# Three late quads instead of four, column ranges of 512, half-block tiles, and a scale moved to GpSimd

## The chip, the cores and the metric

The kernel runs on one core of a Trainium2 chip. The metric is the device time of one execution in microseconds. Each comparison is between medians of several runs; the profile is one further execution, taken by the hardware profiler, and its time is given beside its span.

## The reference

The layer takes 256 positions of width 2048 in float32. What matters here is its second half:

```
hn = rmsnorm(x)                                   # 256 x 2048
x += hier_moe(hn)                                 # 32 experts, each position uses 2 of one group of 8
     # expert e: (silu(xs @ Wg) * (xs @ Wu)) @ w_down[e], w_gate_up[e] 2048 x 1024, w_down[e] 512 x 2048
x += sigmoid(rmsnorm(x) @ w_ple_gate) * (p @ w_ple_proj)      # w_ple_gate 2048 x 2048
y  = rmsnorm(x) * g_final
```

The first half (input projection, attention, short convolution, two branches, output projection) is not touched. All 32 experts' weights are read from memory: 256 MiB of gate/up and 128 MiB of down weights.

## The kernel before, in words

The program is written in engine order by hand: each engine runs its instructions as the Python code issues them, and all weights are fetched by DMAs that SyncE (SP) issues in that order. A load waits on SP until the block of memory that it goes to has been read out by its last user, and every later load waits behind it.

Memory is a set of blocks of 1 MiB (8 KB on each of 128 partitions), named b0 to b25. A list `free` holds those that serve as a rotating ring for weight tiles; `rot_blk` takes the next one, `retire` takes blocks out of the ring for another use.

Experts are worked in quads of four, 32 slots each, so that one quad fills 128 rows (`experts`, line 893). For each expert the gate/up product (`gate_up`, L813) reads 8 tiles of 1 MiB, and `hidden` (L821 to L826) makes the hidden values. In an early quad, `down` (L834) at once reads the expert's four 1 MiB down tiles, and `combine` (L848, L849) places the quad's rows back on the positions and adds them to `x2`. In a late quad (`LATE`, quads 4 to 7) only the hidden values are kept (`tail["hs"]`), with the matrix that places them (`SwT`, in `tail["st"]`); the down products follow in `late_stage` (line 1001).

`late_stage` works by ranges of columns of `x2`, `CHUNKS`: 0 to 1023, 1024 to 1535, 1536 to 2047. For a range, `down_part` loads pieces of w_down for four experts (L1009) and multiplies (L1017), `place` adds the result to `x2` (L1035, L1036), and `prep` (L1050, L140 to L144) transposes the finished columns and splits them into a high and a low part. The range is then a slice of the contraction of `x2 @ w_ple_gate` (class `Gemm`, L262 to L264, three products for each of the two parts). The gate weights are loaded in tiles of four contraction blocks (L230), each split in two halves of two blocks (L140 on ScalarE, L141 on VectorE) into four blocks b14 to b17. `run(n)` issues n such halves, each with the splits for the half three places ahead; 12 matmuls make a half. While one range is multiplied, the down pieces of the next are brought in between the halves.

Quads 4 and 5 (`WIDE`) load pieces of two blocks by 1024 columns, quads 6 and 7 (`FINE`) the same up to column 1023 and pieces of four blocks by 512 columns from there on. All are 1 MiB, and so are most gate tiles.

In the last range the output of the product comes in five lots of columns (three of 512, two of 256). For each lot and both halves of the positions (`g_evac`, L976 to L987): add the sum of the earlier ranges, sigmoid on ScalarE, multiply by the projected embedding, add to `x2`, square on ScalarE for the last norm, and multiply by `g_final` (L987, on VectorE). `store` scales by the last norm's factor and writes out.

Of the kernel before, what the change touches and what calls it, by code (L numbers as in the profile page):

```python
# [37 lines left out]
def block_kernel(  # L38
# [163 lines left out]

    WIDE, FINE = (4, 5), (6, 7)
    LATE = WIDE + FINE
    ex1 = Experts(rot_blk, LATE)

    class Gemm:
        def __init__(self, spool, load):
            self.sp = spool
            self.load = load  # L210
            self.halves = []
            self.ns = 0
            self.nl = 0
            self.i = 0
            self.cur = {}
            self.look = LOOK
            self.feeds = False

        def add(self, src, col, n, ks, acts, evac, before=None):
# [4 lines left out]
        def load_to(self, j):  # L224
            while self.nl < min(j, len(self.halves)):
                src, col, n, ks, k, acts, evac, before, cell = self.halves[self.nl]
                kt = min(4 if n > 256 else 8, ks)
                if k % kt == 0:
                    w = self.load([P, kt, n])
                    SY.dma_start(out=w, in_=src[0, k * P:(k + kt) * P, col:col + n].rearrange(  # L230
                        "(k p) n -> p k n", p=P))
                    cell[k] = w
                self.nl += 1

        def split_to(self, j):
            self.load_to(j)
            while self.ns < min(j, len(self.halves)):
                src, col, n, ks, k, acts, evac, before, cell = self.halves[self.ns]
                kt = min(4 if n > 256 else 8, ks)
# [653 lines left out]
    def experts(ex, first):  # L893
        for q in range(8):
# [6 lines left out]
            for i in range(4):  # L901
# [3 lines left out]
                if first and e == 4 * LATE[0]:  # L905
                    retire(5, 7)
                    tail["hs"] = blk(5, [P, 4 * len(LATE), P])
                    tail["st"] = blk(7, [P, 2, 1024])
# [18 lines left out]
                if i == 0:  # L927
# [3 lines left out]
                    if late:  # L931
                        SwT = tail["st"][:, 0, (q - LATE[0]) * T:(q - LATE[0] + 1) * T]
                    else:
# [7 lines left out]

    CHUNKS = ((0, 1024), (1024, 512), (1536, 512))
    cx = {}

    def cact(c):
# [5 lines left out]
    def late_gate():  # L951
        gg = Gemm(sblk, rot_blk)
        z = []

        def g_evac(c, n, col, w):
            last = c == len(CHUNKS) - 1

            def f(ps):
# [41 lines left out]
    def late_stage(gg):  # L1000
        hs, st = tail["hs"], tail["st"]
        y4c = st[:, 1]
        py = {}

        def down_part(q, col, w, f0, nf):
            tiles = []
            for i in range(4):
                wt = rot_blk([P, nf, w])
                SY.dma_start(out=wt, in_=w_down[0, 4 * q + i, f0 * P:(f0 + nf) * P, col:col + w].rearrange(  # L1009
# [19 lines left out]
        def place(q, col, w):  # L1029
            SwT = st[:, 0, (q - LATE[0]) * T:(q - LATE[0] + 1) * T]  # L1030
            for b in range(w // 512):
# [6 lines left out]
        def prep(c):  # L1038
            o, w = CHUNKS[c]
            if c == 0:  # L1040
                cx[c] = (blk(4, [P, 8, T], FR), blk(Y4, [P, 8, T], FR))
            else:
                hl = blk((18, 4)[c - 1], [P, 2, 4, T], FR)
                cx[c] = (hl[:, 0], hl[:, 1])
            for k in range(0, w // P, 2):
# [22 lines left out]

        prev = None
        for q in LATE:  # L1070
            down_part(q, 0, 1024, 0, 2)
            if prev is not None:
                place(prev, 0, 1024)
            if q == LATE[-1]:
                gg.split_to(3)
            down_part(q, 0, 1024, 2, 2)
            prev = q
        place(prev, 0, 1024)
        prep(0)
        run(4)  # L1080
        for q in WIDE:
            down_part(q, 1024, 1024, 0, 2)
            run(2 if q == WIDE[0] else 1)
            down_part(q, 1024, 1024, 2, 2)
            run(1)
            place(q, 1024, 1024)
            run(1)
        for q in FINE:
            down_part(q, 1024, 512, 0, 4)
            run(1)  # L1090
            place(q, 1024, 512)
            run(1)
        run(15 - gg.i)
        prep(1)
        run(1)
        run(4)
        down_part(FINE[0], 1536, 512, 0, 4)
        run(1)
        place(FINE[0], 1536, 512)
        run(1)  # L1100
        down_part(FINE[1], 1536, 512, 0, 4)
        run(1)
        place(FINE[1], 1536, 512)
        run(1)
        prep(2)
        retire(6)
        gg.load_to(len(gg.halves))
# [127 lines left out]
```

## Time and profile before

| | |
|---|---|
| median of 3 runs | 1738.76 us (1735.45 to 1742.49) |
| profiled execution | 1737.67 us, span 1735.9 us |
| TensorE matmul busy | 1436.4 us, 83% of the span |
| VectorE, ScalarE busy | 594.9 us (34%), 419.9 us (24%) |
| GpSimd busy | 0.6 us |
| moved by DMA | 547.48 MB, mean 315 GB/s |
| chain that ended last | PE 48%, DMA 47% |

How to read it: the mean hides three stages. In the first 600 us TensorE is busy nearly throughout (591.72 of 600 us) and the DMAs move 202 GB/s; from there to the last gate/up product the DMAs are the busier ones; the late stage follows. Shares of a whole span say little about any of these. A matmul's busy time is modelled and pipelined, so the start times of successive rows tell more than the durations.

### The profile page before, as it was taken

What the parts mean: (1) busy time and instruction counts of PE and PEld (TensorE: products, weight loads), DVE (VectorE), ACT (ScalarE), POOL (GpSimd) and SP (SyncE); (2) the same over time, 40 slices, a digit from 0 to 9 for tenths busy, and PEclk for the clock granted to TensorE, in tenths of its full rate; (3) what the DMA queues carried; (4) which work ended last, traced back from release to release, by engine and by line L of the source; (5) the groups of instructions that cost most, each with busy time, mean ns of one, the idle gap of its engine ahead of it and who ended that gap; (6) DMA issues with size and microseconds to landing.
All of it is one profiled execution on the core that took longest, in us unless ns stands there. A gap on an engine that the chain in (4) does not pass through costs nothing.

```text
span 1735.9 us, 22289 instructions
## 1 busy us (share of the span) xinstructions
PE 1436.4 (83%) x9464; PEld 911.1 (52%) x9464; DVE 594.9 (34%) x940; ACT 419.9 (24%) x632; POOL 0.6 (0%) x6
## 2 busy tenths in 40 slices
PE   8999999999999997776676676777876766788993
PEld 6899888888888786332132141243443421134562
DVE  5545766554554544221021030110100100142456
ACT  6434444444444332100000000000100000031244
POOL 0000000000000000000000000000000000000000
PEclk9999999999999999998697797696888777989996
DMA  7656555555557768999999999999999999979961
GB/s 243 202 148 217 194 165 175 182 184 193 192 194 295 263 242 322 411 419 418 420 420 419 419 419 419 419 419 418 419 418 420 419 419 389 391 254 375 387 242 50
DMA packets 147838, 547.48 MB, mean 315 GB/s; under 512 B 13260, under 2 KB 24852, under 8 KB 106260
## 3 DMA queue, kind: packets, MB, share of 16 engines
q1 hardware_dynamic: 147344, 543.85, 81.6%
q10 hardware_dynamic: 388, 2.13, 0.3%
q8 instruction: 76, 1.25, 0.3%
q14 instruction: 30, 0.25, 0.0%
HBM read 543.84 MB, written 2.11 MB: 315 GB/s over the span
## 4 chain that ended last, share of the span: by engine, by line
PE 48%; DMA 47%; DVE 2%; ACT 1%; issue 1%; SPq 0%; ACTq 0%; DVEq 0%
DMA b<-in_w_gate_up_dram 30%; DMA b<-in_w_down_dram 16%; PE acc L262 13%; PE acc L264 13%; PE acc L263 13%; PE tmp L1017 3%; PE acc L813 2%; PE tmp L791 1%; DMA b<-in_w_ple_proj_dram 1%; PE tmp L1035 1%; DMA b<-in_x_dram 0%; PE tmp L655 0%; PE acc L834 0%; DVE b L793 0%; DVE b L984 0%
## 5 line engine op out<-in xcount | busy, mean ns | idle before, releaser
L813 PE MATMUL acc<-b,b 128*32 128x256 f32 x4096 | 325.4, 463 | 132.5 <-DMA b<-in_w_gate_up_dram 107.1
L262 PE MATMUL acc<-b,b 128*128 128x512 f32 (+2 forms) x1096 | 424.7, 388 | 4.7 <-ACT b L140 4.6
L263 PE MATMUL acc<-b,b 128*128 128x512 f32 (+2 forms) x1096 | 413.5, 377 | 1.6 <-DVE b L141 1.6
L264 PE MATMUL acc<-b,b 128*128 128x512 f32 (+2 forms) x1096 | 413.9, 378 | 0.0
L141 DVE TENSOR_TENSOR b<-b,b 128x1024 fp32r<-128x1024 f32 (+2 forms) x278 | 318.2, 1148 | 258.5 <-ACT b L140 257.8
L140 ACT ACTIVATE b<-b 128x1024 fp32r<-128x1024 f32 (+2 forms) x278 | 275.1, 995 | 294.6 <-PE acc L264 266.7
L813 PEld LDWEIGHTS acc<-b,b 128*32 128x32 f32 x4096 | 133.5, 127 | 310.5 <-DMA b<-in_w_gate_up_dram 187.3
L262 PEld LDWEIGHTS acc<-b,b 128*128 128x128 f32 x1096 | 207.3, 189 | 51.1 <-issue 8.7
L263 PEld LDWEIGHTS acc<-b,b 128*128 128x128 f32 x1096 | 207.4, 189 | 38.1 <-DVE b L141 2.3
L264 PEld LDWEIGHTS acc<-b,b 128*128 128x128 f32 x1096 | 207.0, 189 | 37.3 <-DVE b L144 0.2
L821 ACT ACTIVATE hh<-acc 128x128 f32<-128x128 f32 x32 | 8.9, 278 | 577.2 <-PE acc L813 340.6
L822 DVE TENSOR_TENSOR hh<-acc,hh 128x128 f32<-128x128 f32 x32 | 9.3, 291 | 395.6 <-ACT hh L821 395.6
L1017 PE MATMUL tmp<-b,b 128*32 128x512 f32 x512 | 99.7, 705 | 34.6 <-DMA b<-in_w_down_dram 34.6
L834 PE MATMUL acc<-b,hh 128*32 128x512 f32 x512 | 82.0, 757 | 25.8 <-DMA b<-in_w_down_dram 19.8
L791 PE MATMUL tmp<-SS,b 128*128 128x128 f32 x512 | 78.7, 310 | 10.4 <-DVE SS L782 10.4
L791 PEld LDWEIGHTS tmp<-SS,b 128*128 128x128 f32 x512 | 70.6, 215 | 27.4 <-DVE SS L782 12.8
L1017 PEld LDWEIGHTS tmp<-b,b 128*32 128x32 f32 x512 | 21.3, 124 | 107.4 <-DMA b<-in_w_down_dram 64.0
L793 DVE TENSOR_TENSOR b<-tmp,gc 128x512 f32<-128x512 f32 x32 | 22.2, 692 | 126.6 <-PE tmp L791 126.6
L841 DVE COPY b<-acc 32x512 f32<-32x512 f32 x32 | 22.1, 689 | 117.2 <-PE acc L834 116.9
L834 PEld LDWEIGHTS acc<-b,hh 128*32 128x32 f32 x512 | 13.7, 120 | 80.0 <-DMA b<-in_w_down_dram 57.5
L839 ACT ACTIVATE b<-acc 32x512 f32<-32x512 f32 x32 | 18.8, 588 | 103.9 <-PE acc L834 103.7
L825 PE MATMUL tmp<-ident,hh 128*128 128x128 f32 x32 | 11.8, 369 | 36.2 <-DVE hh L823 35.1
(214 smaller groups left out, 602.5 us busy)
## 6 DMA issues: line engine op xcount, KB each, us to landing
b<-in_w_gate_up_dram SPq DMA_DIRECT2D x256, 1024.0 KB, 19.9
b<-in_w_down_dram SPq DMA_DIRECT2D x128, 1024.0 KB, 17.7
b<-in_w_in_dram SPq DMA_DIRECT2D x72, 1024.0 KB, 5.1
b<-in_w_out_dram SPq DMA_DIRECT2D x16, 1024.0 KB, 7.0
b<-in_w_ple_gate_dram SPq DMA_DIRECT2D x15, 1024.0 KB, 13.9
b<-in_w_in_dram SPq DMA_DIRECT2D x12, 688.0 KB, 4.1
b<-in_w_branch_a_dram SPq DMA_DIRECT2D x8, 1024.0 KB, 5.1
b<-in_w_branch_b_dram SPq DMA_DIRECT2D x8, 1024.0 KB, 5.1
```

Of the source, the lines that this page charges most:

```text
L140: S.activation(h, src, AF.Copy)
L141: V.tensor_sub(l, src, h.bitcast(F32))
L262: PE.matmul(o, ah, sb[:, 0, kk, :], start=(k + kk == 0), stop=False)
L263: PE.matmul(o, ah, sb[:, 1, kk, :], start=False, stop=False)
L264: PE.matmul(o, al, sb[:, 0, kk, :], start=False, stop=(k + kk == ks - 1))
L791: PE.matmul(ps[:, c, :], interleaved(xs[t], k), Sr[:, t].rearrange("p e s -> p (e s)"), start=(t == 0), stop=(t == 1))
L793: V.tensor_mul(xg[:, 4 * c4:4 * c4 + 4, :], ps, gc[:, 16 + 4 * c4:20 + 4 * c4].unsqueeze(2).to_broadcast([P, 4, P]))
L813: PE.matmul(gu[32 * j:32 * j + 32, 0:2 * P], xg[:, k, CAP * i:CAP * i + CAP], wv[:, :, P * j:P * j + P], start=(k == 0), stop=(k == KD - 1 ...
L834: PE.matmul(py[c % 2][32 * c:32 * c + 32, :], hT[:, 32 * f:32 * f + 32], wt[:, 512 * c:512 * c + 512], start=(f == 0), stop=(f == 3), tile ...
L839: S.activation(o, py[0][32 * c:32 * c + 32, :], AF.Copy)
L841: V.tensor_copy(o, py[1][32 * c:32 * c + 32, :])
L1017: PE.matmul(pb[32 * i:32 * i + 32, :], hs[:, 4 * (q - LATE[0]) + i, 32 * f:32 * f + 32], tiles[i][:, f - f0, 512 * b:512 * b + 512], start ...
```

## The change

`LATE` becomes quads 5 to 7: quad 4 computes its down products with the early quads. `WIDE` and `FINE` go, and all four ranges are 512 columns wide. Weight tiles of the late stage are half a block, two contraction blocks by 512 columns (four by 256 for the narrow lots): `half_blk` takes nine blocks from the ring and cuts each in two, 18 slots in rotation. One gate tile is then one half of the product (`kt = 1024 // n`). The order of the stage is one function, `bring`: range 0 is brought in without gate product; then, while range c is multiplied, `bring(c + 1, ...)` issues a half after most of its nine steps, seven in all, and one more after `prep(c + 1)`. `prep` now always fills one block, 4 and 23 in turn. Block 18 stays in the ring and block 6 leaves it before expert 29, for `g_final`, whose load moves from the end of the stage to its beginning, on ScalarE's queue. The evacuated down product `y4c` gets the last four column blocks of `hs`. The multiplication by `g_final` goes to GpSimd in all lots but the last.

```
-    WIDE, FINE = (4, 5), (6, 7)
-    LATE = WIDE + FINE
+    LATE = (5, 6, 7)
...
-                kt = min(4 if n > 256 else 8, ks)
+                kt = 1024 // n if self.halved else 4 if n > 256 else 8
...
-                    retire(14, 15, 16, 17, 18, 19, 20)
+                    retire(14, 15, 16, 17, 6, 19, 20)
...
-    CHUNKS = ((0, 1024), (1024, 512), (1536, 512))
+    CHUNKS = tuple((512 * c, 512) for c in range(4))
...
+    def half_blk(shape):
+        n, size = tail.get("halves", 0), 2 * len(free)
+        tail["halves"] = n + 1
+        if n < size and n % 2 == 0:
+            t = rot_blk([P, 2, 1024])
+            ring2.extend(t[:, h] for h in range(2))
+        return ring2[n % size].rearrange("p (k n) -> p k n", k=shape[1])
...
-                    V.tensor_mul(z[t][:, sl], z[t][:, sl], tail["gfb"][:, sl])
+                    (V if n == 4 else G).tensor_mul(z[t][:, sl], z[t][:, sl], tail["gfb"][:, sl])
...
+        def bring(c, between):
+            for q in LATE:
+                for f in (0, 2):
+                    if c == 0 and q == LATE[-1] and f:
+                        gg.split_to(3)
+                    down_part(q, 512 * c, 512, f, 2)
+                    between()
+                place(q, 512 * c, 512)
+                between()
+
+        bring(0, lambda: None)
+        prep(0)
+        for c in range(4):
+            end = gg.i + 8
+            if c < 3:
+                steps = [1, 1, 1, 0, 1, 1, 0, 1, 1]
+                bring(c + 1, lambda: run(steps.pop(0)))
+                prep(c + 1)
+                run(end - gg.i)
         gg.run()
```

On SP, this is the order of loads where range 0 ends, before (the number after b is the block: L1009 are pieces of w_down, L230 gate tiles):

```order
L1009 DMA b24_1179_8940<-in_w_down_dram 128x2x1024
L230 DMA b25_1186_8972<-in_w_ple_gate_dram 128x4x512
L230 DMA b6_1187_8974<-in_w_ple_gate_dram 128x4x512
L1009 DMA b2_1191_8985<-in_w_down_dram 128x2x1024
L1009 DMA b3_1192_8987<-in_w_down_dram 128x2x1024
L1009 DMA b8_1193_8989<-in_w_down_dram 128x2x1024
L1009 DMA b9_1194_8991<-in_w_down_dram 128x2x1024
L230 DMA b10_1209_9080<-in_w_ple_gate_dram 128x4x512
L230 DMA b11_1214_9116<-in_w_ple_gate_dram 128x4x512
L1009 DMA b24_1219_9139<-in_w_down_dram 128x2x1024
L1009 DMA b25_1220_9141<-in_w_down_dram 128x2x1024
L1009 DMA b6_1221_9143<-in_w_down_dram 128x2x1024
```

And the same place in the change, where L1019 is the line of the w_down pieces and x2 stands for both halves of a block:

```order
L1019 DMA b11_1172_8901<-in_w_down_dram 128x2x512 x2
L230 DMA b24_1173_8904<-in_w_ple_gate_dram 128x2x512 x2
L230 DMA b25_1175_8916<-in_w_ple_gate_dram 128x2x512
L1019 DMA b25_1175_8916<-in_w_down_dram 128x2x512
L1019 DMA b18_1176_8919<-in_w_down_dram 128x2x512 x2
L1019 DMA b2_1179_8938<-in_w_down_dram 128x2x512 x2
L1019 DMA b3_1180_8941<-in_w_down_dram 128x2x512 x2
L1019 DMA b8_1182_8953<-in_w_down_dram 128x2x512
L230 DMA b8_1182_8953<-in_w_ple_gate_dram 128x2x512
L1019 DMA b9_1183_8956<-in_w_down_dram 128x2x512 x2
```

Before, block 6 takes the gate tile of the third and fourth half of the product, and the last row, a piece of w_down, goes to that block again. In the change the first three halves have a slot each, the fourth half's tile comes after the first pieces of range 1, and each slot comes up again 18 loads later.

On VectorE, this is the end of the second lot and the start of the third in the last range, before (L987 multiplies by `g_final`, L141 is a split):

```order
L983 TENSOR_TENSOR sgp_1347_9893<-sgp_1347_9893,b13_1009_7741 128x512
L984 TENSOR_TENSOR b20_1217_9134<-b1_656_5373,sgp_1347_9893 128x512
L987 TENSOR_TENSOR b19_1216_9133<-b19_1216_9133,b6_1330_9795 128x512
L987 TENSOR_TENSOR b20_1217_9134<-b20_1217_9134,b6_1330_9795 128x512
L141 TENSOR_TENSOR b17_1350_9906<-b10_1328_9791,b17_1350_9906 128x512
L141 TENSOR_TENSOR b14_1351_9921<-b11_1329_9793,b14_1351_9921 128x512
L976 TENSOR_TENSOR sgp_1352_9936<-acc_1348_9904,b19_1216_9133 128x512
```

And in the change, where the lines are 10 higher:

```order
L993 TENSOR_TENSOR sgp_1304_9940<-sgp_1304_9940,b13_1042_7886 128x512
L994 TENSOR_TENSOR b20_1203_9104<-b1_656_5373,sgp_1304_9940 128x512
L141 TENSOR_TENSOR b17_1307_9953<-b11_1172_8901,b17_1307_9953 128x512
L141 TENSOR_TENSOR b14_1308_9969<-b11_1172_8901,b14_1308_9969 128x512
L986 TENSOR_TENSOR sgp_1309_9984<-acc_1305_9951,b19_1202_9103 128x512
```

The two multiplications (L997 there) now stand on GpSimd, eight in a row with the other lots' and nothing between them; each waits for ScalarE's square of the same tile.

## Rows read from the trace of the kernel before

**Rows 1.** Page, part 2: rate of all DMAs in 40 slices of 43.4 us.
```profile
GB/s 243 202 148 217 194 165 175 182 184 193 192 194 295 263 242 322 411 419 418 420 420 419 419 419 419 419 419 418 419 418 420 419 419 389 391 254 375 387 242 50
```

**Rows 2.** Busy time by stretch, instructions in brackets, TensorE's clock share, DMA share, rate.
```profile
core 0: us, PE busy (x) PEld busy (x) DVE busy (x) ACT busy (x) POOL busy (x), PEclk, DMA share, GB/s
1380.00:1440.00 60.00, 40.31 (x473) 19.05 (x477) 5.04 (x14) 1.67 (x6) 0.00 (x0) 0.83 1.01 418
1444.70:1537.90 93.20, 66.81 (x271) 14.65 (x271) 14.36 (x20) 5.41 (x8) 0.00 (x0) 0.85 1.01 383
1537.90:1548.70 10.80, 10.80 (x50) 4.41 (x51) 3.94 (x6) 1.08 (x3) 0.00 (x0) 0.81 0.56 219
1548.70:1562.70 14.00, 13.19 (x57) 9.21 (x55) 9.85 (x13) 10.77 (x21) 0.00 (x0) 1.00 0.42 124
1562.70:1600.00 37.30, 32.88 (x158) 16.84 (x158) 8.96 (x10) 5.32 (x6) 0.00 (x0) 0.91 1.01 379
1600.00:1640.00 40.00, 35.84 (x175) 17.52 (x173) 12.78 (x16) 7.98 (x10) 0.00 (x0) 1.00 1.04 383
...
1680.50:1735.90 55.40, 27.07 (x128) 21.58 (x126) 34.05 (x71) 27.05 (x55) 0.00 (x0) 0.76 0.19 59
```

**Rows 3.** Timeline of TensorE: start, duration, line, tiles, count [idle before, releaser].
```profile
1444.68 1.93 PE L813 MATMUL acc<-b,b 128*32 128x256 f32 x16 [0.58 <-DMA b<-in_w_gate_up_dram]
...
1537.90 5.66 PE L1017 MATMUL tmp<-b,b 128*32 128x512 f32 x26 [2.47 <-DMA b<-in_w_down_dram]
1543.49 3.70 PE L1035 MATMUL tmp<-b 128*128 128x512 f32 x8
1547.03 1.93 PE L1050 MATMUL tmp<-ident,b 128*128 128x128 f32 x16
1548.72 0.48 PE L262 MATMUL acc<-b,b 128*128 128x512 f32 x1
...
1559.79 1.05 PE L1017 MATMUL tmp<-b,b 128*32 128x512 f32 x4
...
1680.31 1.03 PE L1050 MATMUL tmp<-ident,b 128*128 128x128 f32 x8
```

**Rows 4.** Timeline of the SP queue: start, duration with its waits, count.
```profile
1528.20 28.36 SPq L1009 DMA_DIRECT2D b<-in_w_down_dram  x4
1556.64 0.42 SPq L230 DMA_DIRECT2D b<-in_w_ple_gate_dram  x1
```

**Rows 5.** Waits of the SP queue, 1440 to 1680: total, times, longest.
```profile
SPq L1009 <- DVE b L141: 55.1, 8, 20.5
```

**Rows 6.** Groups by shape, 1548.7 to 1680.3: busy us, mean ns, idle before.
```profile
L1017 PE MATMUL tmp<-b,b 128*32 128x512 f32 x256 | 40.7, 654 | 9.4 <-DMA b<-in_w_down_dram 9.4
L1035 PE MATMUL tmp<-b 128*128 128x512 f32 x32 | 14.7, 592 | 0.0
```

**Rows 7.** Page, part 6: DMA issues, count, KB each, median us to landing.
```profile
b<-in_w_gate_up_dram SPq DMA_DIRECT2D x256, 1024.0 KB, 19.9
...
b<-in_w_ple_gate_dram SPq DMA_DIRECT2D x2, 512.0 KB, 10.8
b<-in_g_final_dram ACTq DMA_DIRECT2D x1, 1024.0 KB, 4.6
```

**Rows 8.** Timeline of VectorE in the last range, between its second and third lot.
```profile
1702.77 0.68 DVE L987 TENSOR_TENSOR b<-b,b 128x512 f32<-128x512 f32 x1
1703.64 0.69 DVE L987 TENSOR_TENSOR b<-b,b 128x512 f32<-128x512 f32 x1 [0.19 <-ACT sgp L985]
1704.25 1.28 DVE L141 TENSOR_TENSOR b<-b,b 128x512 fp32r<-128x512 f32 x2
```

**Rows 9.** Timeline of ScalarE at the same place.
```profile
1702.88 0.63 ACT L985 ACTIVATE sgp<-b 128x512 f32<-128x512 f32 x1 [0.60 <-DVE b L984]
...
1703.51 1.14 ACT L140 ACTIVATE b<-b 128x512 fp32r<-128x512 f32 x2
```

More of the change, by code (lines that the diff above doesn't have):

```diff
@@ L217, in __init__ @@
             self.feeds = False
+            self.halved = False
         def add(self, src, col, n, ks, acts, evac, before=None):
@@ L238, in split_to @@
                 src, col, n, ks, k, acts, evac, before, cell = self.halves[self.ns]
-                kt = min(4 if n > 256 else 8, ks)
+                kt = 1024 // n if self.halved else 4 if n > 256 else 8
                 w = cell[k - k % kt]
@@ L906, in experts @@
                     retire(5, 7)
-                    tail["hs"] = blk(5, [P, 4 * len(LATE), P])
-                    tail["st"] = blk(7, [P, 2, 1024])
+                    tail["hs"] = blk(5, [P, 4 * len(LATE) + 4, P])
+                    tail["sw"] = blk(7, [P, len(LATE), T])
                 if first and e == 19:
@@ L931, in experts @@
                     if late:
-                        SwT = tail["st"][:, 0, (q - LATE[0]) * T:(q - LATE[0] + 1) * T]
+                        SwT = tail["sw"][:, q - LATE[0]]
                     else:
@@ L940, in experts @@
                 combine(SwT, y4, x2)
-    CHUNKS = ((0, 1024), (1024, 512), (1536, 512))
+    CHUNKS = tuple((512 * c, 512) for c in range(4))
     cx = {}
+    ring2 = []
+    def half_blk(shape):
[5 more added lines that the diff above has]
+        return ring2[n % size].rearrange("p (k n) -> p k n", k=shape[1])
     def cact(c):
@@ L951, in late_gate @@
     def late_gate():
-        gg = Gemm(sblk, rot_blk)
+        gg = Gemm(sblk, half_blk)
+        gg.halved = True
         z = []
@@ L1000, in late_stage @@
     def late_stage(gg):
-        hs, st = tail["hs"], tail["st"]
-        y4c = st[:, 1]
+        hs, sw = tail["hs"], tail["sw"]
+        y4c = hs[:, 4 * len(LATE):].rearrange("p e s -> p (e s)")
         py = {}
@@ L1007, in down_part @@
             for i in range(4):
-                wt = rot_blk([P, nf, w])
+                wt = half_blk([P, nf, w])
                 SY.dma_start(out=wt, in_=w_down[0, 4 * q + i, f0 * P:(f0 + nf) * P, col:col + w].rearrange(
@@ L1029, in place @@
         def place(q, col, w):
-            SwT = st[:, 0, (q - LATE[0]) * T:(q - LATE[0] + 1) * T]
+            SwT = sw[:, q - LATE[0]]
             for b in range(w // 512):
@@ L1039, in prep @@
             o, w = CHUNKS[c]
[L1040 to L1044, printed above, removed]
+            hl = blk((4, Y4)[c % 2], [P, 2, 4, T], FR)
+            cx[c] = (hl[:, 0], hl[:, 1])
             for k in range(0, w // P, 2):
@@ L1067, in run @@
             gg.run(gg.i + n)
[L1069 to L1107, printed above, removed]
         tail["gfb"] = blk(6, [P, D])
         S.dma_start(out=tail["gfb"], in_=g_final.rearrange("(o d) -> o d", o=1).broadcast_to([P, D]))
+        def bring(c, between):
[16 more added lines that the diff above has]
+                run(end - gg.i)
         gg.run()
```

## The prediction

> **What bounds the kernel now.** I read the transfer rate over the span first, then the stretches of the last 350 us, then TensorE's timeline at the seams, the SP queue there, and the two engines of the last 50 us. The rate stands at 418 to 420 GB/s from the middle of the span to the end of the experts [rows 1], and a stretch of late experts shows the DMA share at 1.01 with TensorE two thirds busy ([rows 2], 1380 to 1440). The reader should see that up to the last gate/up product at 1444.68 [rows 3] a megabyte moved costs time and a matmul costs none.
>
> After that comes one stage in four pieces. (a) 1444.7 to 1537.9: 32 tiles of w_down for range 0 and two of the gate weights, 34 MiB = 35.65 MB, at 383 GB/s [rows 2]; 35.65 / 0.383 = 93.1 us, so this piece is transfer alone. (b) 1537.9 to 1548.7: last down products, placing, transposes, then the first gate product [rows 3]: 10.8 us at 219 GB/s. (c) 1548.7 to 1680.3: gate products mixed with the other down products. Its first 14 us move only 124 GB/s [rows 2], since the SP queue stands 28.36 us on four loads from 1528.20 on [rows 4]; the longest wait of that queue in the stage is 20.5 us, on the split L141 [rows 5]. The order of the loads explains it: the third of the four loads wants the block of a gate tile whose second half is split only after the first gate product has begun. TensorE then lacks data for 9.4 us in (c) [rows 6] and is busy for the rest. (d) 1680.3 to the end at 1735.9, 55.6 us with almost no transfers: the last range's gate product and the norm, with VectorE busy 34 us.
>
> **The change part by part.** Megabytes are 10^6 bytes; a half tile is 0.524 MB.
>
> *Quad 4 no longer late, ranges of 512.* Sixteen w_down tiles, 16.8 MB, go back among the expert transfers, whose rate is the 418 of [rows 2]: 40.1 us, so the last gate/up product comes at 1484.8. Range 0 then needs 12 experts x 2 half tiles = 12.6 MB, three gate half tiles (1.6) and now also g_final's 1.05 MB, which moved ahead of it: 15.2 MB / 0.383 = 39.7 us. The last load of range 0 lands at 1524.5 instead of 1537.9: **-13.4 us**. In this sum g_final costs 2.7 us; before, it was fetched in piece (d) in 4.6 us [rows 7] beside other work. Its issue stands on ACT behind the last expert's activations and ahead of the first evacuation of a down product; it waits for the readers of block 6, which are through by then, so I charge only its bytes.
>
> *Handover (b).* The down group that follows the last landing has 14 matmuls where 26 took 5.66; placing 4 for 8 (3.70), transposes 8 for 16 (1.93) [rows 3]: 3.05 + 1.85 + 0.97, and 1.6 for the hand-offs between engines, 7.5 instead of 10.8: **-3.3 us**. The gate product starts at 1532.
>
> *Piece (c).* TensorE: 131.6 - 9.4 = 122.2 us of work before. Added: 288 down matmuls for 256 at 40.7/256 = 0.159 (+5.1), 36 placing for 32 at 14.7/32 = 0.46 (+1.8) [rows 6], one more set of transposes (+1.0) [rows 3]; one half of the gate product fewer, since 23 and no longer 24 are run before the last transposes; four took 1548.72 to 1559.79 [rows 3], so -2.8. Sum 127.3. Transfers: 72 + 29 half tiles = 52.9 MB, of which the 8 of the last gate range come after the last w_down; 48.8 MB / 0.383 = 127.4, less the 7.5 of the handover, in which they now run on (the three gate half tiles before GEMM start each have their own slot and are split at once), plus a last down part, two gate halves and a placing (2.5 + 5.5 + 1.8): 129.7. Two limits 2 us apart take turns, so I add 2: 131.7, **+0.1**. That is the point of this change as I read it: the gap goes, and TensorE's own work is what is late next. Lower end: no turns and transfers at 387, 127.3; upper end: as many lost microseconds as today, 127.3 + 9.4 = 136.7.
>
> *Half tiles in 18 slots.* Issues double, at 0.42 us for one [rows 4] against 1.4 us of transfer. Bounds for the rate: 418 (gate/up tiles, 8 KB per partition in one piece) and 379 (1562.7 to 1600) [rows 2]. I take 383, which stands both in (a), with pieces of 4 KB, and at 1600 to 1640, where most loads have the pieces of 2 KB that all will have. A gate/up tile lands 19.9 us after its issue [rows 7], at 418 GB/s eight tiles; a gate tile of 512 KB landed after 10.8 [rows 7], and eight of those on the way carry 388 GB/s, so halving the tile need not starve the queue. The rest of the bookkeeping I cost at nothing: the ring has nine blocks either way (18 stays, 6 leaves), and the evacuated down product only moves into spare columns of the block of hidden values.
>
> The Trainium skill speaks against it: DMA: Bandwidth & Descriptors, section Bandwidth, wants transfers batched to 1 MiB or more, and the fit in its section Anatomy of one DMA, 2.0 us plus bytes over 436 GB/s (for another path of issue), would be (an estimate) 164 GB/s for half a MiB, by which range 0 alone would take 93 us. The same fit gives 238 GB/s for 1 MiB, where [rows 2] show 418, so the fixed part is covered here by the transfers behind it.
>
> *The extra half behind the last transposes.* One half of the third range now runs after them, ahead of the last range's product: 2.8 us of TensorE, and two adds on VectorE. Part may hide behind the norm that the first lot waits for; I charge all: **+2.8**.
>
> *Multiplication on GpSimd.* VectorE loses 2 x 0.69 us in each of three lots. In lot 1 they run from 1702.77 to 1704.25, and the split L141 starts there [rows 8]. But its other input comes from ACT's L140, which starts at 1703.51 behind L985 and needs half of 1.14 us: ready at 1704.1 [rows 9]. So the two multiplications fill a wait, and taking them off gains 0.15 us in that lot. No row shows a GpSimd multiplication. Below, it could gain VectorE's whole 3 x 1.4 = 4.1 us if ACT were early; above, if GpSimd takes twice VectorE's 0.69 and holds L141 back for both, 2.8 - 1.3 = 1.5 us a lot, 4.5 in all. L141's wait on ACT is the nearest row: I take **0**. Behind a multiplication on GpSimd stand only the next ones; the scaling by the last norm waits for them, a lot and a norm later.
>
> Sum: -13.4 - 3.3 + 0.1 + 2.8 = -13.8. The profiled execution took 1737.67 (span 1735.9), so 1723.9; the median of the runs, 1738.76, is 1.1 higher. I put the forecast at **1724.5**.
>
> **The rivals.**
>
> *Turns cost as much as today (A).* TensorE and the transfers in (c) differ by 2 us over 130, and each group of four loads must land whole before its matmuls begin. If that costs 9.4 us again, (c) is 136.7: +5.0 more, and with a rate of 379 in all, 64 MB, +1.8: 1731. For: the same 9.4 in [rows 6] with bigger buffers of the same bytes. Against: most of it follows the gap.
>
> *Half tiles move slower (B, the other side).* 64 MB (15.2 + 48.8) go through them. At 383 that is 167.1 us. The gain of 13.8 is gone at 64 / 180.9 = 354 GB/s, and slower by half a per cent below 64 / 189.6 = 338. With 330, 193.9 us: 1751. Place: the SP queue, every load from the end of the experts on. For it: from the expert stretch to (a) the rate falls from 418 to 383 [rows 2], so the shape of a load matters. Against: it falls no further at 1600 to 1640, with shorter pieces. The page's rule on 1 MiB, above, points here too; its figure would be far beyond this rival's, and its fit misses the 1 MiB loads of this trace.
>
> *GpSimd holds VectorE (C).* As bounded above, +4.5: 1729. For it: nothing else in the tail is as tight as VectorE. The Trainium skill, SBUF — State Buffer, section Who interferes with whom, says that a VectorE operation with two SBUF inputs and a GpSimd operation that reads SBUF exclude each other for a whole instruction; L141, L983 and L984 are of that kind. No run here shows it yet. If it holds, L141 starts after both GpSimd multiplications, and the lots grow instead of shrinking.
>
> *The gap closes, TensorE runs without waits and the half tiles move at 418 (D).* Then (c) is 127.3, 4.4 less, and range 0 takes 36.4 instead of 39.7: 1717. It is the same side.
>
> **How the numbers follow.** Half a per cent, 8.7 us, is about what a measurement of this kernel can tell from no change: faster is below 1730.1, slower above 1747.5. Forecast with D 0.62 (own range 1714 to 1731, the upper end (c)'s 136.7 and a little; faster but for 0.02); C 0.14 (0.10 faster, 0.04 same); A 0.15 (0.02 faster, 0.13 same); B 0.09 (0.01 same, 0.08 slower). Faster 0.72, same 0.20, slower 0.08. Low end 1711: D with GpSimd's gain of 4.1, 1713, and the extra half partly hidden. High end 1737: A and C together, 1724.5 + 6.8 + 4.5 = 1736.
>
> **What would show it.** Right: the last gate/up product near 1485, the first gate product near 1532, no stretch of 10 us below 300 GB/s between them and the last w_down, the last transposes near 1664, and a tail of 58 us. The handover is wrong if the rate falls there. (c) is wrong if TensorE's idle time on w_down is far above 5 us or if the rate is below 370. GpSimd's part is wrong if L141 waits for anything but L140, or if the last norm waits for GpSimd. The forecast fails as a whole if the rate of the half tiles falls below 354 GB/s.

## The result and the profile after

The changed kernel takes **1723.21 us** (median of four runs, 1721.6 to 1724.09) against 1739.09 before (four runs beside it, 1735.45 to 1742.49): ratio 0.9908, interval 0.9887 to 0.9929. Its profiled execution took 1721.6, with a span of 1719.8 us. The forecast was 1724.5.

Page, part 2, of the changed kernel: the rate in 40 slices, now of 43.0 us.

```profile
GB/s 243 205 149 221 196 149 176 191 190 191 184 194 275 268 265 303 393 418 419 419 419 419 420 419 418 419 419 418 419 419 420 419 419 419 369 385 386 385 244 51
```

The slice at 254 GB/s of [rows 1] is gone. One slice of 369 stands where the experts end, and after it 385 or so until the last loads.

The stretches that answer to [rows 2], cut at the last gate/up product, the first gate product and the last transposes, with two windows of 10 us about the handover (columns as there):

```profile
1485.40:1533.90 48.50, 35.94 (x150) 8.79 (x150) 10.84 (x17) 6.18 (x11) 0.00 (x0) 0.89 1.02 366
...
1520.00:1530.00 10.00, 7.61 (x20) 1.57 (x20) 3.19 (x4) 1.44 (x2) 0.00 (x0) 0.83 1.05 386
1530.00:1540.00 10.00, 9.47 (x55) 4.54 (x55) 3.96 (x7) 3.72 (x9) 0.00 (x0) 1.00 1.05 385
...
1533.90:1661.50 127.60, 125.38 (x605) 68.98 (x602) 58.61 (x78) 36.10 (x57) 0.00 (x0) 1.00 1.04 383
1661.50:1719.80 58.30, 31.64 (x141) 26.25 (x139) 33.78 (x64) 27.91 (x56) 10.08 (x8) 0.74 0.14 39
```

In the 127.6 us between the product and the transposes the DMA share is 1.04 from end to end and TensorE is busy for 125.38 us. Both look full; the experiments tell which is the limit. In the handover, where before had 219 GB/s, the rate is 385. TensorE's timeline at the seams, for [rows 3]:

```profile
1485.38 1.07 PE L813 MATMUL acc<-b,b 128*32 128x256 f32 x16 [0.79 <-DMA b<-in_w_gate_up_dram]
...
1521.40 5.95 PE L1027 MATMUL tmp<-b,b 128*32 128x512 f32 x16 [3.51 <-DMA b<-in_w_down_dram]
...
1528.35 1.99 PE L1045 MATMUL tmp<-b,b 128*128 128x512 f32 x4 [0.99 <-DVE b L1037]
...
1531.11 0.98 PE L1057 MATMUL tmp<-ident,b 128*128 128x128 f32 x7 [0.53 <-DVE b L1046]
1532.03 1.92 PE L1027 MATMUL tmp<-b,b 128*32 128x512 f32 x16
1533.88 0.50 PE L262 MATMUL acc<-b,b 128*128 128x512 f32 x1
...
1661.48 1.03 PE L1057 MATMUL tmp<-ident,b 128*128 128x128 f32 x8
```

Between the transposes and the first gate product stands a down part of range 1 (1532.03, 1.92 us). The groups of this stretch of 127.6 us, for [rows 6], and SP's waits on `g_final` and on a split between 1470 and 1670, for [rows 5]:

```profile
L1027 PE MATMUL tmp<-b,b 128*32 128x512 f32 x276 | 43.7, 599 | 2.2 <-DMA b<-in_w_down_dram 1.8
L1045 PE MATMUL tmp<-b,b 128*128 128x512 f32 x36 | 16.9, 591 | 0.0
```

```profile
SPq L1019 <- DMA b<-in_g_final_dram: 7.5, 1, 7.5
...
SPq L1019 <- DVE b L141: 0.3, 1, 0.3
```

SP's 55.1 us of waiting on splits are down to 0.3, and TensorE's idle time on `w_down` from 9.4 to 1.8. A new wait came, 7.5 us on `g_final`, a load that ScalarE (ACT) issues. The chain of waits from the last gate/up tiles on (start, duration, what):

```profile
1465.30 20.04 DMA b<-in_w_gate_up_dram
1488.11 9.11 DMA b<-in_g_final_dram
...
1540.34 10.78 DMA b<-in_w_down_dram
1551.16 1.90 PE tmp L1027 x10
...
1561.99 10.74 DMA b<-in_w_down_dram
...
1583.62 11.59 DMA b<-in_w_down_dram
...
1597.99 10.78 DMA b<-in_w_down_dram
...
1635.91 4.56 PE tmp L1027 x32
...
1641.29 10.98 DMA b<-in_w_down_dram
1652.31 1.90 PE tmp L1027 x10
```

Up to 1609 it goes through transfers for the most part, with TensorE between 1551 and 1562; from 1609 to 1641 and from 1652 on it goes through TensorE. The chain by itself thus does not say which of the two is the limit either.

In all kernels below, G is the start of the last gate/up product, P that of the first gate product, T that of the last transposes, all read as above, and E the span's end. G differs by some 3 us between kernels that are alike up to there, so the pieces are compared. Each ratio is to runs of the kernel before that were made beside that kernel's; their medians lie between 1739.1 and 1739.5.

| kernel | median us | ratio to before (interval) | G to P | P to T | T to E |
|---|---|---|---|---|---|
| before | 1739.1 | | 104.0 | 131.6 | 55.6 |
| after | 1723.2 | 0.9908 (0.9887 to 0.9929) | 48.5 | 127.6 | 58.3 |
| three late quads alone | 1741.1 | 1.0009 (0.9999 to 1.0019) | 80.3 | 114.6 | 55.6 |
| before, fourth half split early | 1727.8 | 0.9931 (0.9914 to 0.9949) | 103.9 | 122.0 | 55.3 |
| after, tiles of 1 MiB | 1732.7 | 0.9967 (0.9955 to 0.9979) | 55.7 | 131.4 | 58.5 |
| the same, fourth half split early | 1724.7 | 0.9919 (0.9903 to 0.9936) | 55.1 | 120.8 | 58.5 |
| after, four late quads | 1724.4 | 0.9913 (0.9896 to 0.9929) | 59.8 | 162.2 | 56.4 |
| after, two late quads | 1725.0 | 0.9913 (0.9896 to 0.9929) | 37.6 | 99.7 | 57.4 |
| after, third product left out | 1723.0 (one run) | | 48.1 | 127.4 | 58.3 |
| after, 9.4 MB fewer | 1708.7 (one run) | | 48.3 | 113.8 | 58.5 |
| after, all scaling on VectorE | 1720.8 | 0.9896 (0.9881 to 0.9910) | 47.6 | 127.9 | 56.2 |
| after, `g_final` late | 1719.8 | 0.9888 (0.9872 to 0.9905) | 45.1 | 127.5 | 58.3 |
| combined | 1717.6 | 0.9874 (0.9857 to 0.9890) | 44.9 | 126.8 | 55.8 |
| combined, eight steps | 1717.4 | 0.9873 (0.9857 to 0.9890) | 45.6 | 128.5 | 54.8 |

The first two pieces can be compared only between kernels with the same number of late quads; quad 4's bytes wander between them.

### The profile page after: what moved, and what is told of

Same layout as the page of the kernel before. It is cut to its first block, busy times and chain, and to the rows that moved or that the text cites. A ratio compares the mean times of both kernels' runs of the same rounds, so it can differ in the third digit from the quotient of the medians.

```text
span 1719.8 us, 22466 instructions
## 1 busy us (share of the span) xinstructions
PE 1426.0 (83%) x9464; PEld 908.1 (53%) x9464; DVE 602.0 (35%) x950; ACT 423.7 (25%) x642; POOL 10.6 (1%) x14
## 4 chain that ended last, share of the span: by engine, by line
DMA 49%; PE 44%; issue 3%; DVE 2%; ACT 1%; SPq 0%; ACTq 0%; DVEq 0%
DMA b<-in_w_gate_up_dram 30%; DMA b<-in_w_down_dram 15%; PE acc L262 13%; PE acc L264 13%; PE acc L263 12%; DMA b<-in_w_ple_gate_dram 2%; DMA b<-in_w_ple_proj_dram 1%; PE tmp L1027 1%; PE acc L813 1%; PE tmp L791 1%; PE acc L834 1%; DMA b<-in_g_final_dram 1%; DMA b<-in_x_dram 0%; PE tmp L655 0%; PE tmp L1045 0%
## 5 line engine op out<-in xcount | busy, mean ns | idle before, releaser
L813 PE MATMUL acc<-b,b 128*32 128x256 f32 x4096 | 321.5, 459 | 138.2 <-DMA b<-in_w_gate_up_dram 112.9
L141 DVE TENSOR_TENSOR b<-b,b 128x1024 fp32r<-128x1024 f32 (+2 forms) x278 | 320.6, 1156 | 253.2 <-ACT b L140 252.0
L140 ACT ACTIVATE b<-b 128x1024 fp32r<-128x1024 f32 (+2 forms) x278 | 275.2, 995 | 275.2 <-PE acc L264 247.8
L834 PE MATMUL acc<-b,hh 128*32 128x512 f32 x640 | 102.0, 753 | 32.1 <-DMA b<-in_w_down_dram 24.7
L791 PEld LDWEIGHTS tmp<-SS,b 128*128 128x128 f32 x512 | 70.5, 215 | 29.0 <-DVE SS L782 15.6
L1027 PE MATMUL tmp<-b,b 128*32 128x512 f32 x384 | 70.7, 625 | 10.2 <-DMA b<-in_w_down_dram 9.8
L841 DVE COPY b<-acc 32x512 f32<-32x512 f32 x40 | 27.6, 689 | 146.0 <-PE acc L834 145.6
L839 ACT ACTIVATE b<-acc 32x512 f32<-32x512 f32 x40 | 23.5, 587 | 129.3 <-PE acc L834 129.0
L1027 PEld LDWEIGHTS tmp<-b,b 128*32 128x32 f32 x384 | 14.8, 111 | 58.2 <-DMA b<-in_w_down_dram 33.7
L848 PE MATMUL acc<-b,SS 128*128 128x512 f32 x80 | 39.5, 650 | 3.4 <-ACT b L839 3.4
## 6 DMA issues: line engine op xcount, KB each, us to landing
b<-in_w_down_dram SPq DMA_DIRECT2D x96, 512.0 KB, 10.8
b<-in_w_ple_gate_dram SPq DMA_DIRECT2D x32, 512.0 KB, 10.8
```

Source lines behind the costliest of these rows:

```text
L140: S.activation(h, src, AF.Copy)
L141: V.tensor_sub(l, src, h.bitcast(F32))
L791: PE.matmul(ps[:, c, :], interleaved(xs[t], k), Sr[:, t].rearrange("p e s -> p (e s)"), start=(t == 0), stop=(t == 1))
L813: PE.matmul(gu[32 * j:32 * j + 32, 0:2 * P], xg[:, k, CAP * i:CAP * i + CAP], wv[:, :, P * j:P * j + P], start=(k == 0), stop=(k == KD - 1 ...
L834: PE.matmul(py[c % 2][32 * c:32 * c + 32, :], hT[:, 32 * f:32 * f + 32], wt[:, 512 * c:512 * c + 512], start=(f == 0), stop=(f == 3), tile ...
L839: S.activation(o, py[0][32 * c:32 * c + 32, :], AF.Copy)
```

## The experiments

### Which part of the change gains: the gap, the ranges, the half tiles

**Three late quads alone**, in the kernel before:

```
-    WIDE, FINE = (4, 5), (6, 7)
+    WIDE, FINE = (5,), (6, 7)
```

> The kernel before with three late quads (5 wide, 6 and 7 fine) and nothing else changed: ranges of 1024, 512, 512, tiles of 1 MiB. Theory (a late quad costs TensorE 14 us in the stage behind range 0 and 22 us of transfer in range 0, and moves 40 us of transfer to the experts; the gap stays): +40.1 - 21.9 - 13.9 = +4, 1743. Rival (three late quads are the gain): 1730 or less.

Measured 1741.1, no gain. From the first gate product to the last transposes:

```profile
1566.40:1681.00 114.60, 107.10 (x515) 66.15 (x513) 51.35 (x63) 36.80 (x56) 0.00 (x0) 0.99 0.86 312
```

A DMA share of 0.86: the gap stays, and quad 4's bytes, which moved to the front, no longer follow it.

**One number in the kernel before**: four halves of the first gate product instead of three are split ahead of it. The third and the fourth share a tile, whose block becomes free with the fourth's split.

```
             if q == LATE[-1]:
-                gg.split_to(3)
+                gg.split_to(4)
```

> The kernel before with one number changed: four halves of the gate product are split ahead of range 0's last down part instead of three, so that both gate tiles leave their blocks early. Theory (the gap at 1540 to 1560 comes from one block held by a half that is not split): the rate there rises from 94 to 151 GB/s to above 300, SP's wait of 20.5 us on L141 is gone, TensorE's idle time on w_down falls from 9.4 us to 2 to 4, time 1731 to 1734. Rival (TensorE's own work sets the end, and groups of four 1 MiB tiles make it wait anyway): the gap closes but the time stays at 1738 to 1739.

Measured 1727.8: 11.5 us of the change's 15.9 by one number, more than I expected. Its windows over the old gap and near the end of its loads, and its group of down products in P to T:

```profile
1540.00:1550.00 10.00, 10.00 (x48) 4.38 (x40) 3.94 (x6) 1.41 (x3) 0.00 (x0) 0.83 1.02 386
1550.00:1560.00 10.00, 10.00 (x45) 8.26 (x44) 6.30 (x10) 7.45 (x16) 0.00 (x0) 1.00 0.87 332
1560.00:1570.00 10.00, 10.00 (x60) 5.74 (x58) 3.63 (x4) 3.21 (x5) 0.00 (x0) 1.00 0.84 274
...
1650.00:1660.00 10.00, 10.00 (x56) 5.83 (x48) 4.65 (x7) 2.39 (x3) 0.00 (x0) 1.00 0.58 214
...
L1017 PE MATMUL tmp<-b,b 128*32 128x512 f32 x256 | 35.4, 622 | 5.0 <-DMA b<-in_w_down_dram 5.0
```

Where [rows 2] show 219 and 124 GB/s, the rate is 386 and 332, and 274 in the 10 us behind. The block whose second half was split only after the gate product had begun held up the queue; splitting it earlier frees it. Not all went as expected: SP's longest wait on a split is still 10.3 us and not gone, and TensorE idles 5.0 us on `w_down`, not 2 to 4.

Some transfer time is still lost here. The three windows at 332, 274 and 214 GB/s move 8.2 MB where 383 would move 11.5, which is 8.6 us (an estimate). The one at 1650 is a second gap of the same kind, near the last loads of `w_down`: SP stands 8.8 us on a split. The kernel before has it too, as SP's waits on splits between 1640 and 1681 show (total, times, longest):

```profile
SPq L1009 <- DVE b L141: 15.1, 3, 8.8
```

**The change with tiles of 1 MiB**, so that the third and fourth half share a block again (with one down part per expert quad, the table of steps becomes [2, 1, 1, 1, 1, 1]):

```
-        gg = Gemm(sblk, half_blk)
-        gg.halved = True
+        gg = Gemm(sblk, rot_blk)
...
-                for f in (0, 2):
-                    if c == 0 and q == LATE[-1] and f:
-                        gg.split_to(3)
-                    down_part(q, 512 * c, 512, f, 2)
-                    between()
+                if c == 0 and q == LATE[-1]:
+                    gg.split_to(3)
+                down_part(q, 512 * c, 512, 0, 4)
+                between()
```

> The changed kernel with tiles of 1 MiB in the same nine blocks: pieces of four contraction blocks by 512 columns, gate tiles for two halves of the product, everything else as changed. Theory (a whole gate tile holds its block until its second half is split, behind the start of the gate product, and SP stands meanwhile): SP waits about 20 us on L141 once, a stretch of 10 us or more below 250 GB/s follows the start of the gate product, TensorE's idle time on w_down grows from 2 to 7 to 11 us, time 1728 to 1732. Rival 1 (the tile size does not matter with ranges of 512): 1723. Rival 2 (transfers of 1 MiB are more efficient): below 1720.

Measured 1732.7, 0.7 above the expected range, and the gap is back (windows, then SP's waits):

```profile
1530.00:1540.00 10.00, 8.48 (x46) 2.74 (x42) 2.29 (x4) 1.16 (x3) 0.00 (x0) 0.83 0.51 190
1540.00:1550.00 10.00, 10.00 (x57) 6.00 (x48) 3.01 (x5) 2.95 (x7) 0.00 (x0) 1.00 0.37 111
...
SPq L230 <- DVE b L141: 17.9, 1, 17.9
```

**The same with `gg.split_to(4)`**:

> The whole-tile version of the changed kernel with one more number: four halves of the gate product are split early, not three. Theory (the half tiles gain by the gap alone: no block is held by half a tile that is not split): SP's wait of 17.9 us and the stretch at 111 to 190 GB/s go, time 1723 to 1726, as the changed kernel. Rival (half tiles also feed TensorE in finer groups, which whole ones cannot): the gap closes, but TensorE still waits 7 us or more for w_down between first gate product and last transposes, 1728 or more.

Measured 1724.7, 8.0 less, an interval of the ratio that overlaps the change's own. Its window at 1480, for later, and P to T of this kernel:

```profile
1480.00:1490.00 10.00, 6.29 (x57) 1.87 (x51) 0.58 (x2) 0.56 (x2) 0.00 (x0) 0.78 0.92 342
...
1541.10:1661.90 120.80, 116.00 (x589) 67.74 (x586) 56.89 (x75) 35.07 (x55) 0.00 (x0) 1.00 1.02 375
```

So the four kernels agree: a full block waiting for its second split costs 8 to 11 us, with either size of range, and tiles of half a block remove that wait and give nothing else that these intervals can tell. The rate from P to T, 375 against 348 in "before, fourth half split early", shows that most of what that kernel still lost is won with tiles of 1 MiB too. Three late quads alone do not win it: SP waits 24.8 us on splits between 1640 and 1681 there. That points at the ranges of 512 with their order of loads, which no run tries by themselves.

**Four and two late quads**, the rest as in the change (with four, `y4c` moves to `sw` and three steps are added; with two, six steps issue seven halves):

```
-    LATE = (5, 6, 7)
+    LATE = (4, 5, 6, 7)      # the other: (6, 7)
-                steps = [1, 1, 1, 0, 1, 1, 0, 1, 1]
+                steps = [1, 1, 1, 0, 1, 0, 0, 1, 1, 0, 1, 1]   # the other: [1, 1, 1, 1, 1, 2]
```

> The changed kernel with four late quads (4 to 7) again; ranges of 512, half tiles and the rest as changed, with 12 steps between the halves instead of 9. Theory (between late and early, a quad's 16.8 MB only changes the rate at which they move, 383 instead of 418 GB/s, as long as TensorE has time): last gate/up product 40 us earlier, range 0 11 us longer, the stretch from first gate product to last transposes 33 us longer (160) and bound by transfers with TensorE idle 15 us or more; 3.7 us slower than the changed kernel, 1727. Rival (the number of late quads is what the change gains by): 1735 or more.

> The changed kernel with two late quads (6 and 7), else as changed. Theory (now TensorE is the limit of the late stage and the transfers idle): last gate/up product 40 us later, range 0 11 us shorter, the stretch from first gate product to last transposes 109 us by TensorE instead of 128 (transfers would need 95): 11 us slower, 1734, with the rate in that stretch below 340 GB/s. Rival (fewer late products are always better, since the experts' rate is higher): 3.7 us faster, 1719.5.

Measured 1724.4 and 1725.0, both expectations too slow (1727 and 1734) and neither kernel apart from the change. P to T, with four, then with two late quads and its down products:

```profile
1505.50:1667.70 162.20, 156.37 (x724) 79.03 (x721) 66.62 (x89) 38.31 (x61) 0.00 (x0) 1.00 1.03 379
```

```profile
1565.90:1665.60 99.70, 99.70 (x496) 62.01 (x493) 54.47 (x69) 35.30 (x54) 0.00 (x0) 1.00 0.99 364
...
L1027 PE MATMUL tmp<-b,b 128*32 128x512 f32 x180 | 23.2, 599 | 0.0
```

With four late quads TensorE idles on `w_down` for 5.7 us instead of the 15 and more that I expected. With two it shows no idle time, and a down matmul costs 23.2 / 180 = 0.129 us. The 0.158 of the change (43.7 / 276) and the 0.159 of the prediction thus hold time in which matmuls wait for data and count as busy. That made my sum for TensorE too long, here and in the expectation for two late quads.

### What limits the stretch from P to T

**Less work for TensorE**: of the three products of each contraction block, the third is left out in the late gate products.

```
-                        PE.matmul(o, ah, sb[:, 1, kk, :], start=False, stop=False)
-                        PE.matmul(o, al, sb[:, 0, kk, :], start=False, stop=(k + kk == ks - 1))
+                        PE.matmul(o, ah, sb[:, 1, kk, :], start=False, stop=(self.halved and k + kk == ks - 1))
+                        if not self.halved:
+                            PE.matmul(o, al, sb[:, 0, kk, :], start=False, stop=(k + kk == ks - 1))
```

> The changed kernel without the third of the three products of the late gate product (low part of the activations times high part of the weights is left out); all loads, splits and down products as they are. 92 matmuls of 0.227 us, 20.9 us of TensorE's work, leave the stretch between first gate product and last transposes. If TensorE's own work is late there, as predicted, the stretch shrinks from 127.6 to between 107 and 115. If transfers set it, it stays at 126 to 128 and TensorE shows idle time on w_down of 10 us and more.

**Fewer bytes**: in ranges 1 to 3 the fourth expert's pieces of w_down are left out, and its products use the third expert's.

```
+                if col and i == 3:
+                    tiles.append(tiles[-1])
+                    continue
```

> The changed kernel with the fourth expert's w_down pieces of ranges 1 to 3 not loaded (its products use the third expert's piece); all matmuls as they are. 18 half tiles, 9.4 MB, 24.6 us of transfer leave the stretch between first gate product and last transposes. If transfers set it, the stretch shrinks from 127.6 to TensorE's own time: 118, from the two-quad version's 99.7 plus 96 down matmuls at its 0.129 and 12 placings at 0.47. If TensorE's work sets it, it stays above 125.

P to T of the two and their down products, without the third product and with fewer bytes:

```profile
1535.60:1663.00 127.40, 119.66 (x513) 53.50 (x510) 56.29 (x78) 35.90 (x57) 0.00 (x0) 1.00 1.05 384
...
L1028 PE MATMUL tmp<-b,b 128*32 128x512 f32 x276 | 59.1, 601 | 7.7 <-DMA b<-in_w_down_dram 7.7
```

```profile
1534.60:1648.40 113.80, 113.80 (x604) 67.19 (x601) 58.50 (x78) 36.10 (x57) 0.00 (x0) 1.00 0.95 348
...
L1030 PE MATMUL tmp<-b,b 128*32 128x512 f32 x276 | 32.1, 596 | 0.0
```

Some 90 matmuls fewer, and the stretch stays at 127.4 at 384 GB/s. With 18 half tiles fewer (9.4 MB) it is 113.8, without a pause of TensorE and at 348 GB/s. So transfers set 127.6, and TensorE's own work is at most 113.8, some 14 us below. Each kernel ran once, but the stretches stand far outside what kernels alike up to there differ by.

The same 276 down matmuls show 59.1 us, 43.7 in the change and 32.1 here: 0.214, 0.158 and 0.116 us each. The more they must wait for data, the more they count as busy, so the first kernel shows only 7.7 us of idle time and not the 10 and more that I expected. The expectation of 118 for the second was 4 too high, since its 0.129 from the two late quads held waits too. Of TensorE's 125.38 busy us in the change, 11.6 at least are matmuls that wait.

### `g_final` and GpSimd

**`g_final` late**: the two lines that load it move from the start of `late_stage` to just ahead of its last `gg.run()`.

> The changed kernel with the load of g_final issued where it was before, ahead of the last range's product; block 6 is kept free for it as changed. Three theories of the low rate at 1480 to 1510 (326 to 364 GB/s) and the 7.5 us that SP waits there. Wait: the queue runs low because SP waits for g_final's landing; rate at 383 there and the megabyte gone, first gate product 5 to 6 us earlier, 1717.5. Bytes only: the low rate belongs to the change of tile shape and stays, first gate product 2.7 us earlier, 1720.5. Hidden anyway: no change, 1723.

Measured 1719.8; G to P is 3.4 us shorter. Windows of 10 us from 1480 on, after and then this kernel:

```profile
1480.00:1490.00 10.00, 7.13 (x54) 2.22 (x55) 0.58 (x2) 0.55 (x2) 0.00 (x0) 0.67 0.93 326
1490.00:1500.00 10.00, 6.13 (x22) 1.35 (x24) 0.00 (x0) 0.00 (x0) 0.00 (x0) 0.84 0.94 346
```

```profile
1480.00:1490.00 10.00, 6.63 (x64) 2.19 (x64) 0.47 (x2) 0.28 (x1) 0.00 (x0) 0.66 0.92 343
1490.00:1500.00 10.00, 8.82 (x32) 1.95 (x33) 0.11 (x1) 0.28 (x1) 0.00 (x0) 0.83 1.03 373
```

SP's wait on `g_final` is gone, and the share at 1490 goes from 0.94 to 1.03. A dip to 343 remains. It is not the half tiles' doing: the kernel with tiles of 1 MiB and the fourth half split early has 342 in the same window. Three late quads with the old ranges of 1024 have 411 there; why the dip comes was not tried. Of the 3.4 us, 2.7 are the bytes; the other 0.7 is within what such a stretch can tell (G to P is 47.6 to 48.5 in four kernels that are alike up to there), so most of SP's 7.5 us was covered by loads on the way.

**All scaling on VectorE**:

```
-                    (V if n == 4 else G).tensor_mul(z[t][:, sl], z[t][:, sl], tail["gfb"][:, sl])
+                    V.tensor_mul(z[t][:, sl], z[t][:, sl], tail["gfb"][:, sl])
```

> The changed kernel with all multiplications by g_final back on VectorE, all else as changed. Theory (a GpSimd multiplication shuts out VectorE's split L141, whose inputs both lie in SBUF, until it ends): the pairs of L141 between lots take about 1.3 to 1.8 us again instead of 1.8 to 2.4, the first three lots take 9.05, 6.9 and 6.3 us instead of 9.55, 7.7 and 7.1, the fourth 3.65 instead of 2.65, so the tail is 1.2 us shorter: about 1722. Rival 1 (GpSimd relieves VectorE): the tail grows by the 5 us of multiplications, 1728. Rival 2 (the splits are long for another reason, such as the half tiles): L141 keeps its length and the time stays within 0.5 us of 1723.

Measured 1720.8; the interval of its ratio overlaps the change's, but T to E is 2.1 us shorter, 1.4 of it up to the last norm. The ends of the second and third lot, VectorE and GpSimd of the change, then the end of the second on VectorE with all scaling on it:

```profile
1685.27 0.69 DVE L994 TENSOR_TENSOR b<-b,sgp 128x512 f32<-128x512 f32 x1
1687.28 2.22 DVE L141 TENSOR_TENSOR b<-b,b 128x512 fp32r<-128x512 f32 x2 [1.31 <-ACT b L140]
...
1695.00 1.59 DVE L141 TENSOR_TENSOR b<-b,b 128x512 fp32r<-128x512 f32 x1 [1.31 <-ACT b L140]
```

```profile
1685.47 2.88 POOL L997 TENSOR_TENSOR b<-b,b 128x512 f32<-128x512 f32 x2 [5.39 <-ACT sgp L995]
1693.20 2.84 POOL L997 TENSOR_TENSOR b<-b,b 128x512 f32<-128x512 f32 x2 [4.85 <-ACT sgp L995]
```

```profile
1686.08 0.69 DVE L994 TENSOR_TENSOR b<-b,sgp 128x512 f32<-128x512 f32 x1
1686.69 0.68 DVE L997 TENSOR_TENSOR b<-b,b 128x512 f32<-128x512 f32 x1
1687.56 0.69 DVE L997 TENSOR_TENSOR b<-b,b 128x512 f32<-128x512 f32 x1 [0.19 <-ACT sgp L995]
1688.17 1.29 DVE L141 TENSOR_TENSOR b<-b,b 128x512 fp32r<-128x512 f32 x2
```

On VectorE the multiplications fill the wait for ScalarE, and the two splits take 1.29 us, from 1.40 us after the last L994. On GpSimd that wait stands empty, the splits start 1.32 us after it, 0.08 earlier, and take 2.22: this lot loses 0.9. In the third lot one split ends 0.55 us after GpSimd (1696.59 and 1696.04), where it takes 0.69 with all scaling on VectorE. The rival that blamed half tiles for the long splits is out: with the same tiles they are short again.

**Combined**: `g_final` late, and GpSimd only in lot n = 3, the next to last, which is 256 wide.

```
-                    (V if n == 4 else G).tensor_mul(z[t][:, sl], z[t][:, sl], tail["gfb"][:, sl])
+                    (G if n == 3 else V).tensor_mul(z[t][:, sl], z[t][:, sl], tail["gfb"][:, sl])
```

> The changed kernel with g_final loaded late and only the fourth lot's multiplication on GpSimd, the first three and the fifth on VectorE. Theory: the gains of both add, 2.7 to 5.5 us at the front and 2 us in the tail: 1716 to 1718.5. Rival (front and tail hide each other's gain or neither is real): 1721 to 1723.

Measured 1717.6: both gains add up. Each of its four runs is faster than every run of either kernel, though the intervals of the ratios still overlap. In the fourth lot GpSimd seems to help: from the last transposes to the last norm it is 39.8 us, and 40.6 with all scaling on VectorE (one profile of each). Against "before, fourth half split early" the combined kernel is 10.2 us faster, with intervals that do not overlap; the 8.6 us estimated there would be most of that, but no run tries them alone. **Eight steps**: in the last range the last half of the product ahead of the transposes stands among the last down parts, and one fewer follows them.

```
-                steps = [1, 1, 1, 0, 1, 1, 0, 1, 1]
+                steps = [1, 1, 1, 0, 1, 1, 1 if c == 2 else 0, 1, 1]
```

> The combined version (g_final late, only the fourth lot's multiplication on GpSimd) with the last half of the third range issued among the last down parts instead of behind the last transposes. Theory (TensorE has slack among the down parts, and the half delays the first lot by 1.5 us behind the transposes): last transposes at most 1 us later, first lot 1.5 us sooner after them, 1716.5 to 1717. Rival (TensorE has no slack there): transposes 2.8 us later, the sum 1 us slower than the combined version's 1717.6.

Measured 1717.4, no difference that can be told: P to T is 1.7 longer, T to E 1.0 shorter, which is between the theory and its rival. Whether that half costs anything where it stands is left open.

## Why the prediction was right, and where not

**The time and the gap held.** 1723.2 against 1724.5, and the cause of the gain is the one read from [rows 4, 5]: a gate tile's block, held until its second half was split, behind which the queue stood. Undoing it by one number gains 11.5 us in the kernel before and 8.0 in the change with tiles of 1 MiB, and half tiles gain 9.5 there.

**Piece (a)** held: last gate/up product 1485.38 (1484.8 forecast), last landing of range 0 at 1525.4 (1524.5; the load is issued at 1514.28 and lands 11.1 us later). `g_final`, charged with its bytes at 2.7, cost 3.4 in G to P.

**The handover** came out at 1533.88 instead of 1532. Besides the later landing, it took 8.5 us and not 7.5: I did not count that a down part of range 1 stands ahead of the first gate half (1.85 us up to the gate product). The two waits for evacuations, 0.99 and 0.53, are the 1.6 that I had, and the down matmuls after the landing were shorter, 1.9 instead of 3.05.

**Piece (c): time nearly right, step wrong.** "TensorE's own work is what is late next" was wrong. The step sized TensorE at 127.3 with a price of 0.159 per down matmul, taken from a stretch in which those matmuls waited for data. With fewer bytes to wait for they cost 0.116, and the whole is at most 113.8. The transfer side of the same sum is what happened: from P to the last landing of `w_down` (1641.29 and 10.98 later) it is 118.4 us, where I had 127.4 - 7.5 = 119.9, and from there to the last transposes 9.2, where I had 9.8. The 2 us for turns were not there: TensorE, some 14 us ahead, has nothing to trade turns with. So 131.7 was 4.1 too long, which made up for the 1.9 missed in the handover and more: that the sum came so close is partly luck. The lower end, 127.3, was TensorE's sum again; transfers at 387 with the same two ends make 128.4.

**Rivals A, B and D.** TensorE's idle time on `w_down` is 1.8 and not 9.4 (A), and the rate is not 418 (the further gain in D). Half tiles kept their rate: 383 in P to T, each landing 10.8 us after its issue, as [rows 7] had it for two of them. B, with 330, did not happen. The Trainium skill, DMA: Bandwidth & Descriptors, section Bandwidth, asks for 1 MiB or more per transfer; measured here, 1 MiB tiles without the gap give 375 GB/s in P to T and half tiles 383, so that advice did not decide.

**The tail** held in sum, 58.3 against 55.6 + 2.8 = 58.4, but by two errors that cancelled, which is luck. The extra half cost less: from the last transposes to VectorE's first add of the first lot it was 9.2 us before (1680.31 to 1689.52) and is 10.7 now (1661.48 to 1672.14), +1.5 instead of +2.8. And GpSimd's multiplication is not free: from the first add to the last norm it was 30.0 us before, is 31.3 now, and is 30.0 again with the multiplication back on VectorE, so it costs 1.4. The rest of the 2.1 gained there lies behind the norm, where the code is the same (16.4, 16.3 and 15.6 us in the three kernels). Rival C was right in its mechanism and had 0.14, but its 4.5 us was three times what came. I took the value nearest to a row on ScalarE's wait and gave the unknown operation's length too little weight. The sign that I named, L141 waiting for anything but L140, could not show it: the row still names L140, and the time lost to GpSimd stands in the split's own 2.22 us. The rows show GpSimd taking 1.44 us for what VectorE does in 0.69, and the pair of splits that overlaps it ending 1.15 us after GpSimd does (1689.50, 1688.35): an undisturbed pair takes 1.29, so hardly any of it ran beside GpSimd. The Trainium skill, SBUF — State Buffer, section Who interferes with whom, says that a VectorE operation with both inputs in SBUF contends with a GpSimd operation that reads SBUF, for ports held by one at a time; this trace agrees.

**Three late quads** were credited with the bulk of -13.4. The accounting by bytes is right, but quad 4's bytes only change place: with two, three or four late quads the time is 1725.0, 1723.2 and 1724.4, and alone, on the kernel before, the change from four to three gains nothing. What my sum booked under (a) as gained by moving quad 4 was the gap, filled. The sum could not tell, since it compared landings and not the lost transfer time of [rows 2]: before, 24.8 us at 219 and 124 GB/s instead of 383, which is 14.1 us lost. That figure was there to be read, and is about the whole gain forecast. The second gap, near the last loads of `w_down`, I did not see at all.

## What to carry to other kernels

When a queue feeds everything, first add up the transfer time lost in its gaps and find which buffer's reader holds it; here one number that freed a buffer earlier was worth 11.5 of this change's 15.9 us. Test which of two full engines is the limit by taking work from each, because waiting matmuls count as busy. Work moved off a busy engine gains nothing where it filled a wait, and costs where, as here, the first engine's next operations hardly ran beside it.

## What was not expected of the hardware

- A load on ACT's queue held SP's loads: 7.5 us of SP's waiting went to `g_final`, which SP doesn't use at that place, and moving the load ended it. Why SP's order waits for it was not tried.
- A down matmul shows 0.158 us of busy time in a stretch limited by transfers, 0.214 when TensorE has less other work there, and 0.116 with fewer bytes to wait for.
- The same 128x512 multiplication takes 1.44 us on GpSimd (2.88 for two) and 0.69 on VectorE, and a pair of splits that starts beside it 2.22 us instead of 1.29.
- Half tiles of 512 KB kept 383 to 386 GB/s; the gate/up tiles, 1 MiB, 418.
